# First weight chunk and x in smaller pieces on two DMA queues, with products on zeros during the loads

## Chip, cores and metric

The kernel runs on one core of a Trainium2 chip. The metric is the device time of one execution in microseconds (us).

## What is computed

One step of a two-layer decoder trunk for a prompt of 256 tokens and 8 sample tokens, 264 columns together, with 1024 features. Layer 0 mixes tokens by retention, layer 1 by a gated linear recurrence; each layer then has cross attention over a memory and a convolutional feed-forward block. All is float32. Only the beginning matters here:

```python
def trunk(x, offset, ret_s, ...):
    for i in range(DEPTH):
        hn = rmsnorm(x, p['norm_mix'][i])
        if i % N_MIXERS == 0:
            y, s = retention_mixer(hn, ret_s[j], offset, p['ret_w_in'][j], p['ret_w_out'][j])
        ...
        x = x + y
        x = x + cross_attn(rmsnorm(x, p['norm_xa'][i]), mem_k[i], mem_v[i], ...)
        y, fb = conv_ffn(rmsnorm(x, p['norm_ffn'][i]), ...)
        x = x + y

def retention_mixer(h, s0, offset, w_in, w_out):
    q, k, v, g = jnp.split(h @ w_in, [nqk, 2 * nqk, 2 * nqk + nv], axis=-1)
    ...
```

## The kernel before

Features lie on the 128 partitions, tokens along the columns. An output tile of a projection is 128 features by 264 tokens, and its sum runs over eight row tiles of 128 input features. To keep float32 precision every operand is split into two parts of fewer bits: a weight chunk `wraw` (128 x 1024 values, one output tile with its eight row tiles) is copied by ScalarE into the rounded part `wh` (`cp`, L333) and VectorE subtracts to get the rest, `wl` (`tt`, L293). The input of a projection is split in the same way: `gain` scales one row tile of x by the norm's gains on ScalarE into `A[0]` (L329) and VectorE makes the rest, `A[1]` (L299). One row tile then is three products (`mm3`): wh with the first part of A, wh with the second, wl with the first. A chunk is 24 products.

The weights form one stream of chunks, loaded through SyncE's DMA queue into six slots (`fetch`, `load` L350) and split into four slots of wh and wl (`split_next`). A load into a slot waits until the chunk in it has been split.

The order of nearly all instructions is chosen when the kernel is built: class `Clock` keeps a rough time for each engine, and a greedy planner (`one`, `process`, `until`) places background work (splits, norms, attention, stores) between the products of the main stream by these times. The main stream's order is fixed by the list `items`.

The beginning is written out by hand. `start` issues the loads and the first splits and scalings, and adds the first norm's work `g` as a background task. The first unit after it is `K.pair(*qkv[0][:2], 4)`: two output tiles, here called a (chunk 0) and b (chunk 1), in the order rows 0 to 3 of a, rows 0 to 3 of b, rows 4 to 7 of a, rows 4 to 7 of b, 48 products. Ahead of `start`, VectorE fills and copies a zeroed piece of the buffer `kvt`. The norm's factor is not needed for these products; it is multiplied in later.

Of the kernel before, what the change touches and what calls it, by code (L numbers as in the profile page):

```python
# [10 lines left out]
F32 = mybir.dt.float32  # L11
# [8 lines left out]
P = 128  # L20
D = 1024
T = 256
# [12 lines left out]

# [1 line left out]
_PRM = {}  # L37
# [17 lines left out]

# [1 line left out]
C_ID, C_ONE, C_COS, C_SIN, C_MASK = 0, P, 2 * P, 2 * P + NT, 2 * P + 3 * NT  # L57
# [113 lines left out]
class Clock:  # L171
    """A rough model of the engines' queues, by which the order of the instructions is chosen."""

# [78 lines left out]
class Kern:  # L252
# [9 lines left out]

# [1 line left out]
    @staticmethod  # L264
# [11 lines left out]
    def mm_col(self, out, lhsT, rhs, j, start, stop):  # L276
        """A product with 32 stationary columns, in column tile j of the array; four of them run side by side."""
        self.c.op("pe", 24.0 if j else max(214.0, 4 * self._n(rhs) / 2.4 + 3.0), [out], [lhsT, rhs], start)
        self.nc.tensor.matmul(out, lhsT, rhs, start=start, stop=stop, tile_position=(0, LO * j))  # L279
# [59 lines left out]
    def gain(self, m, x, g):  # L339
        """Rows x of feature tile m times its gains, split into self.A; the second half of the work returned."""  # L340
        self.act(self.A[0][:, m, :], x, AF.Identity, scale=g)
        return lambda: self.stt(self.A[1][:, m, :], x, g, self.A[0][:, m, :].bitcast(F32), MUL, SUB)
# [14 lines left out]

# [1 line left out]
    def get(self, n):  # L359
# [55 lines left out]
    def rebank(self, n):  # L415
        """From now on n banks for the main stream, the others for the background."""
        self.mgoal = n
        while self.mtot < n and self.aux:
            self.mtot += 1
            self.main.append(self.aux.popleft())  # L420
        while self.mtot > n and self.main:
            self.mtot -= 1
            self.aux.append(self.main.popleft())

# [1 line left out]
    def set_stream(self, units):  # L426
# [14 lines left out]
    def split_at(self):  # L441
        """When the next chunk of the stream can be split, as far as that is known."""
        while self.nsplit < self.nload and self.chunks[self.nsplit].raw:
            self.nsplit += 1
        if self.nsplit == self.nload or not self.hfree:
            return None
        t = max(self.chunks[self.nsplit].at, self.c.used(self.wh[:, self.hfree[0], :]))
        return max(t, self.calm(self.nsplit))

    def calm(self, n):  # L450
        """When chunk n of the stream, which is not the next to be used, may get in the way of other work."""
        d = n - self.cur
        if d < 2:
            return 0.0
        w = self.patience[min(d - 2, 1)]
        return max(self.c.t["dve"], self.c.t["act"]) - w
# [23 lines left out]
    def need(self, c):  # L480
        """Chunk c is the next of the stream to be used."""
        self.cur += 1
        self.fetch_all()
        self.until(lambda: c.rslot is not None)
        if not c.raw:
            while c.hslot is None:
                self.until(lambda: self.split_at() is not None or c.hslot is not None)
                if c.hslot is None:
                    self.split_next()
            if c.low:  # L490
                self.resume(c.low, self.now)
# [28 lines left out]

# [1 line left out]
    def add(self, gen, prio=1, at=None):  # L522
# [121 lines left out]

# [1 line left out]
    def proj(self, src, src_rhs, evac, n=NT, parts=False, tag=None):  # L646
        """The chunks in src hold the rows of one 128-feature tile, in order; with parts a unit each."""
        st = {}
# [30 lines left out]
    def pair(a, b, cut=6):  # L679
        """Two projections of one chunk each, with the last rows of the contraction of both at the end."""  # L680
        first = []
# [21 lines left out]

# [1 line left out]
    def newton(self, a, y, n, root=False):  # L705
        """y = a ** -0.5: a first guess from the exponent bits, or the root from a table, then Newton steps."""
        t = self.get(n)
# [13 lines left out]
    def rsqrt_mean(self, sq, n, cnt, wide=False, tok=None, root=False):  # L721
        """[128, n] copies of (column sums of sq / cnt + EPS) ** -0.5; a generator that returns them."""
        b = yield from self.wbank()
# [41 lines left out]
    def norm_later(self, wide=False):  # L765
        """The factors of the norm over what self.sq holds, as self.r, a few steps on."""
        gen = self.gen
# [15 lines left out]

# [1 line left out]
    def mem_units(self, l):  # L785
# [95 lines left out]

# [1 line left out]
    def retention(self):  # L883
# [237 lines left out]
    def ret_update(self, heads):  # L1121
        """New retention states of the samples: gamma * state + k v^T."""
        order = [(h, s) for h in heads for s in range(S)]
# [77 lines left out]

# [1 line left out]
    def residual(self, gain, scale=False):  # L1203
        """What becomes of the sums of output tile m: they are added to x."""
        self.gen += 1
# [48 lines left out]
    def blocks(self, plan, rows, evac):  # L1254
        """A unit for each (chunk, tiles, k): the chunk holds rows k, ... of the contraction for some output tiles."""
        bank, units, seen = {}, [], {}
# [22 lines left out]

# [1 line left out]
    def xattn(self, l):  # L1281
# [34 lines left out]
    def parts(self, src, dims):  # L1316
        """A copy of src in two parts of fewer bits that add up to it."""
        n = self._n(src)
# [73 lines left out]
    def bcast(self, src, n0):  # L1392
        """Two rows of src, n0 and n0 + 1, on all partitions of a bank."""
        b = yield from self.wbank()
# [11 lines left out]
    def samples(self, b, w, kind, l, h):  # L1406
        """Rows 32 (s % 4) + s of bank b: column s of w[:, :, s, :] times block s of the cache, over both halves."""
        ps = self.ps[:, b, :256]
# [15 lines left out]
    def gather(self, b, rows):  # L1424
        """Column s of half t of bank b: row 32 (s % 4) + s of columns 128 t to 128 t + 127 of rows."""
        for t in range(2):
# [68 lines left out]

# [1 line left out]
    def ffn(self, l):  # L1497
# [62 lines left out]

# [1 line left out]
    def lru_prep(self):  # L1562
        # 8 log_sigmoid(lam) = 8 (min(lam, 0) - log1p(exp(-|lam|))), log1p(z) = 2 artanh(z / (2 + z))
        lam = self.par[:, _PRM["lru_lambda"]:_PRM["lru_lambda"] + KD]
# [21 lines left out]
    def lru(self):  # L1586
# [3 lines left out]
        def half(name, m, n=4):  # L1590
            """Feature tile m of a buffer that is kept for half of the tiles."""
            k = (name, m // 4)
# [152 lines left out]

# How eager each part of the program is, in us: patience (2), slack of the task kinds 1 to 3, tilt, ahead.
POLICY = (
# [6 lines left out]
def tile_hybrid_step(ctx: ExitStack, tc: tile.TileContext, ins, outs):  # L1754
# [88 lines left out]
    def start():  # L1843
        K.fetch()
        nc.scalar.dma_start(out=K.par[:, :NG], in_=ins["par"][:, :NG])
        K.load(K.x[:, :4, :], ins["x"][:, :4, :])
        K.fetch()
        K.load(K.x[:, 4:, :], ins["x"][:, 4:, :])
        K.fetch()
        K.load(K.cst[:, :C_MASK], ins["cst"][:, :C_MASK])  # L1850

        def split():
            c = K.chunks[K.nsplit]
            K.split_next()
            K.resume(c.low, K.now)
        split()
        K.load(K.cst[:, C_MASK:], ins["cst"][:, C_MASK:])
        K.load(K.par[:, NG:], ins["par"][:, NG:])
        for m in range(KD):
            K.gain(m, K.x[:, m, :], K.prm("norm_mix", m))()  # L1860
            K.ready.add(("A", 0, m))
            if m == 3:
                split()
        split()

# [35 lines left out]
    def staged(units, n):  # L1901
        """The last part of each of the first n tiles comes after the other parts of all of them."""
        out = [u for us in units[:n] for u in us[:-1]] + [us[-1] for us in units[:n]]
        return out + [u for us in units[n:] for u in us]
# [9 lines left out]
    def out(w, plan, rows, gain):  # L1914
        """plan: what to wait for, or chunks of w."""
        ev = K.blocks([c for st in plan if isinstance(st, list) for c in st], rows, K.residual(gain))
# [131 lines left out]
```

## Time and profile before

| | us |
|---|---|
| median of 3 runs | 1046.58 |
| lowest and highest run | 1046.05 to 1047.74 |
| span of the profiled execution (first to last instruction) | 1044.7 |
| own time of the profiled execution | not listed apart from the three runs |
| TensorE busy | 1023.0 |
| VectorE busy | 807.4 |
| ScalarE busy | 589.4 |

The profiled execution is one run of the program recorded by the hardware profiler. Its span leaves out what lies before the first and after the last instruction; the median is 1.9 us above it. PE is TensorE's matmul, PEld its weight load, DVE is VectorE, ACT ScalarE, SP SyncE; L274 is line 274 of the kernel. The ends of matmuls are modelled, so the distance between the starts of two rows tells their pace better than their durations do.

### The profile page before, as it was taken

How to read it: one execution, taken by the hardware profiler on the slowest of the kernel's cores; microseconds unless marked ns; L12 is line 12 of the kernel's file. 1: busy time of each engine (PE TensorE's matmuls, PEld its weight loads, DVE VectorE, ACT ScalarE, POOL GpSimd, SP SyncE). 2: the span in 40 equal slices, each digit the busy share in tenths (PEclk: the TensorE clock that was granted, in tenths of full speed). 3: DMA queues.
4: the chain of work that ended last, by engine and by line, in shares of the span. 5: the costliest groups of instructions: out<-in, count | busy, mean ns of one | idle time of the engine just before them, and what ended most of it. 6: DMA issues, size and time to landing. Idle time of an engine off the chain costs nothing.

```text
span 1044.7 us, 20974 instructions
## 1 busy us (share of the span) xinstructions
PE 1023.0 (98%) x8158; PEld 966.4 (93%) x8158; DVE 807.4 (77%) x1685; ACT 589.4 (56%) x979; POOL 84.4 (8%) x190
## 2 busy tenths in 40 slices
PE   7999999999999999999999999999999999999996
PEld 7988999889998868999999999999878999999996
DVE  7968788777677644898988776989755898898773
ACT  6554555455545434575676554697444666766552
POOL 0000000000000000023221000400000222121000
PEclk9999999999999999999999999999999999999998
DMA  9667766774766897567888977546886668777851
GB/s 371 207 216 248 272 224 232 263 262 164 271 218 235 297 315 256 191 212 259 266 297 291 301 235 233 172 164 233 311 286 223 209 203 290 272 256 272 299 192 62
DMA packets 70916, 255.45 MB, mean 245 GB/s; under 512 B 8096, under 2 KB 8736, under 8 KB 70304
## 3 DMA queue, kind: packets, MB, share of 16 engines
q1 hardware_dynamic: 70384, 253.53, 70.4%
q8 instruction: 64, 1.05, 0.4%
q10 hardware_dynamic: 432, 0.58, 0.2%
q14 instruction: 36, 0.29, 0.1%
HBM read 229.34 MB, written 24.74 MB: 243 GB/s over the span
## 4 chain that ended last, share of the span: by engine, by line
PE 87%; DVE 6%; DMA 3%; ACT 3%; issue 1%; SPq 0%; DVEq 0%; ACTq 0%
PE ps L274 83%; PE ps L279 3%; DVE wl L293 2%; DVE x L299 2%; DVE x L293 1%; DMA kvt<-in_cache_v 1%; DMA x<-in_cache_k 1%; ACT x L329 1%; PE ps L289 1%; ACT L329 1%; ACT wh L333 1%; DMA kvt<-in_cache_k 1%; DVE x L318 0%; DMA wraw<-in_ret_w_in 0%; DVE B L293 0%
## 5 line engine op out<-in xcount | busy, mean ns | idle before, releaser
L274 PE MATMUL ps<-A,wh 128*128 128x264 f32 x2816 | 525.1, 287 | 7.1 <-ACT A L329 6.3
L333 ACT CAST wh<-wraw 128x1024 fp32r<-128x1024 f32 x284 | 297.2, 1049 | 281.3 <-PE ps L274 237.2
L274 PEld LDWEIGHTS ps<-A,wh 128*128 128x128 f32 x2816 | 437.2, 189 | 16.0 <-ACT A L329 6.3
L293 DVE TENSOR_TENSOR wl<-wraw,wh 128x1024 fp32r<-128x1024 f32 x296 | 359.2, 1220 | 93.4 <-ACT wh L333 85.6
L274 PE MATMUL ps<-A,wl 128*128 128x264 f32 x1408 | 400.1, 284 | 0.1
L274 PE MATMUL ps<-B,wh 128*128 128x264 f32 (+1 forms) x1664 | 311.8, 288 | 2.2 <-DVE B L293 2.2
L274 PEld LDWEIGHTS ps<-B,wh 128*128 128x128 f32 x1664 | 257.3, 188 | 12.7 <-issue 8.6
L274 PEld LDWEIGHTS ps<-A,wl 128*128 128x128 f32 x1408 | 265.1, 188 | 0.4 <-DVE wl L293 0.3
L274 PE MATMUL ps<-B,wl 128*128 128x264 f32 (+1 forms) x832 | 235.5, 283 | 0.0
L274 PEld LDWEIGHTS ps<-B,wl 128*128 128x128 f32 x832 | 156.2, 188 | 0.0
L293 DVE TENSOR_TENSOR x<-ps,x 128x264 f32<-128x264 f32 (+2 forms) x248 | 83.9, 364 | 33.1 <-PE ps L274 21.2
L337 POOL COPY x<-x 128x16 f32<-128x16 f32 (+2 forms) x162 | 78.3, 518 | 268.1 <-DVE x L293 217.2
L329 ACT ACTIVATE x<-x 128x264 f32<-128x264 f32 (+4 forms) x166 | 59.7, 389 | 20.2 <-DVE x L293 8.7
L299 DVE SCALAR_TENSOR_TENSOR x<-x,par 128x280 f32<-128x280 f32 (+3 forms) x128 | 61.5, 488 | 2.3
L333 ACT COPY x<-ps 128x512 f32<-128x512 f32 (+3 forms) x85 | 39.2, 475 | 42.0 <-PE ps L274 31.2
L299 DVE SCALAR_TENSOR_TENSOR kvt<-x,vst,kvt 128x256 f32<-128x256 f32 x128 | 53.3, 477 | 1.3 <-ACT kvt L329 1.3
L299 DVE SCALAR_TENSOR_TENSOR junkt<-kvt,x 128x256 bf16<-128x256 f32 x128 | 46.4, 420 | 9.1 <-DMA kvt<-in_state_ret 6.4
L293 DVE TENSOR_TENSOR x<-x 128x264 f32<-128x264 f32 (+6 forms) x106 | 44.8, 435 | 7.7 <-ACT x L329 5.8
L333 ACT CAST B<-x 128x264 fp32r<-128x264 f32 (+2 forms) x84 | 34.7, 417 | 24.5 <-DVE x L293 17.4
L329 ACT ACTIVATE x<-x,par 128x280 f32<-128x280 f32 (+2 forms) x64 | 38.6, 605 | 8.9 <-DVE x L293 5.9
L293 DVE TENSOR_TENSOR B<-x,B 128x264 fp32r<-128x264 f32 (+2 forms) x84 | 36.7, 438 | 8.4 <-ACT B L333 8.2
L274 PE MATMUL ps<-wh,B 128*128 128x512 f32 x128 | 42.5, 400 | 0.0
(100 smaller groups left out, 703.6 us busy)
## 6 DMA issues: line engine op xcount, KB each, us to landing
wraw<-in_ffn_w_up SPq DMA_DIRECT2D x96, 512.0 KB, 4.4
kvt<-in_state_ret SPq DMA_DIRECT2D x64, 512.0 KB, 6.0
wraw<-in_ret_w_in SPq DMA_DIRECT2D x48, 512.0 KB, 4.4
wraw<-in_ffn_w_down SPq DMA_DIRECT2D x48, 512.0 KB, 4.7
out_ret_s<-kvt SPq DMA_DIRECT2D x32, 512.0 KB, 5.1
x<-in_cache_v SPq DMA_DIRECT2D x18, 512.0 KB, 6.7
wraw<-in_xa_w_k SPq DMA_DIRECT2D x16, 512.0 KB, 4.4
wraw<-in_xa_w_v SPq DMA_DIRECT2D x16, 512.0 KB, 4.1
```

Of the source, the lines that this page charges most:

```text
L274: self.last = self.nc.tensor.matmul(out, lhsT, rhs, start=start, stop=stop)
L279: self.nc.tensor.matmul(out, lhsT, rhs, start=start, stop=stop, tile_position=(0, LO * j))
L289: self.nc.tensor.transpose(out, in_, self.ident[:n, :n])
L293: self.nc.vector.tensor_tensor(out=out, in0=a, in1=b, op=op)
L299: self.nc.vector.scalar_tensor_tensor(out, a, s, b, op0, op1, **kw)
L329: self.nc.scalar.activation(out, in_, func, **kw)
L333: self.nc.scalar.copy(out, in_)
L337: self.nc.gpsimd.tensor_copy(out, in_)
```

## The change

In `start`, five float32 products of 128 x 128 with 128 x 256 on a zeroed part of `kvt` are put ahead of everything, into a PSUM bank that nothing uses then. Chunk 0 is loaded in three pieces (row tiles 0 and 1, 2 and 3, 4 to 7), x in three (row tiles 0 and 1 through ScalarE's queue; 2 and 3, then 4 to 7 through SyncE's). The pieces of chunk 0 are split one by one, each followed by the scalings of its row tiles of x. Chunks 1 and 2 are split after that. Chunk 1 is now issued behind all of x, and the constants go ahead of chunk 2. The pair's order is the same. The rest of the diff removes comments.

```diff
     def start():
-        K.fetch()
+
+        zero = kvt[:, 0, :512]
+        nc.vector.memset(zero, 0.0)
+        for _ in range(5):
+            K.mm(K.ps[:, 7, :256], zero[:, :P], zero[:, P:P + 256], True, True, False)
+        c = K.chunks[0]
+        c.rslot, c.hslot = K.rfree.popleft(), K.hfree.popleft()
+        K.nload = K.nsplit = 1
+        cuts = (0, 256, 512, 1024)
+        parts = [slice(a, b) for a, b in zip(cuts, cuts[1:])]
+        raw, wh, wl = (t[:, n, :] for t, n in ((K.wraw, c.rslot), (K.wh, c.hslot), (K.wl, c.hslot)))
         nc.scalar.dma_start(out=K.par[:, :NG], in_=ins["par"][:, :NG])
-        K.load(K.x[:, :4, :], ins["x"][:, :4, :])
-        K.fetch()
+        K.load(raw[:, parts[0]], c.src[:, parts[0]])
+        nc.scalar.dma_start(out=K.x[:, :2, :], in_=ins["x"][:, :2, :])
+        K.load(raw[:, parts[1]], c.src[:, parts[1]])
+        K.load(K.x[:, 2:4, :], ins["x"][:, 2:4, :])
+        c.at = K.load(raw[:, parts[2]], c.src[:, parts[2]])
         K.load(K.x[:, 4:, :], ins["x"][:, 4:, :])
         K.fetch()
         K.load(K.cst[:, :C_MASK], ins["cst"][:, :C_MASK])
-
-        def split():
+        K.fetch()
+        m = 0
+        for n, p in enumerate(parts):
+            K.cp(wh[:, p], raw[:, p])
+            K.tt(wl[:, p], raw[:, p], wh[:, p].bitcast(F32), SUB)
+            for m in range(cuts[n] // P, cuts[n + 1] // P):
+                K.gain(m, K.x[:, m, :], K.prm("norm_mix", m))()
+                K.ready.add(("A", 0, m))
+        K.rfree.append(c.rslot)
+        K.fetch()
+        K.load(K.cst[:, C_MASK:], ins["cst"][:, C_MASK:])
+        K.load(K.par[:, NG:], ins["par"][:, NG:])
+        for _ in range(2):
             c = K.chunks[K.nsplit]
             K.split_next()
             K.resume(c.low, K.now)
-        split()
-        K.load(K.cst[:, C_MASK:], ins["cst"][:, C_MASK:])
-        K.load(K.par[:, NG:], ins["par"][:, NG:])
-        for m in range(KD):
-            K.gain(m, K.x[:, m, :], K.prm("norm_mix", m))()
-            K.ready.add(("A", 0, m))
-            if m == 3:
-                split()
-        split()
```

## Rows read from the trace of the kernel before

**Rows 1.** The page, busy us of each engine, share of the span, instructions.

```profile
PE 1023.0 (98%) x8158; PEld 966.4 (93%) x8158; DVE 807.4 (77%) x1685; ACT 589.4 (56%) x979; POOL 84.4 (8%) x190
```

**Rows 2.** The chain that ended last: start us, us, what.

```profile
7.05 27.24 PE ps L274 x206
```

**Rows 3.** TensorE's waits: us in total, times, longest us.

```profile
PE ps L274 <- ACT A L329: 6.3, 1, 6.3
PE ps L274 <- DVE B L293: 2.2, 2, 1.7
PE ps L274 <- DVE sq L293: 1.9, 1, 1.9
PE ps L279 <- DMA x<-in_cache_k: 1.7, 2, 1.4
PE ps L274 <- DVE x L299: 1.3, 1, 1.3
```

**Rows 4.** Windows: length, busy us by engine, granted clock, DMA share, GB/s.

```profile
0.00:5.00 5.00, 0.00 (x0) 0.00 (x0) 1.94 (x3) 2.00 (x2) 0.20 (x4) 1.00 0.62 222
5.00:10.00 5.00, 3.54 (x14) 3.24 (x15) 4.15 (x7) 4.20 (x9) 0.00 (x0) 1.00 1.01 394
...
12.00:300.00 288.00, 288.00 (x2145) 270.20 (x2143) 224.05 (x583) 148.89 (x236) 3.01 (x5) 1.00 0.71 249
```

**Rows 5.** Timeline of TensorE: start us, us, instruction, [idle before it <- releaser].

```profile
6.30 0.59 PE L274 MATMUL ps<-A,wh 128*128 128x264 f32 x1 [6.30 <-ACT A L329]
7.05 0.59 PE L274 MATMUL ps<-A,wh 128*128 128x264 f32 x1 [0.16 <-DVE A L299]
...
11.02 0.64 PE L274 MATMUL ps<-A,wh 128*128 128x264 f32 x2
11.46 0.35 PE L274 MATMUL ps<-A,wl 128*128 128x264 f32 x1
...
12.00 0.41 PE L274 MATMUL ps<-A,wh 128*128 128x264 f32 x2
...
14.93 0.41 PE L274 MATMUL ps<-A,wh 128*128 128x264 f32 x2
```

**Rows 6.** Timeline of ScalarE.

```profile
4.28 1.04 ACT L333 CAST wh<-wraw 128x1024 fp32r<-128x1024 f32 x1 [1.83 <-DMA wraw<-in_ret_w_in]
5.73 1.73 ACT L329 ACTIVATE A<-x,par 128x264 fp32r<-128x264 f32 x4 [0.40 <-DMA x<-in_x]
7.62 1.05 ACT L333 CAST wh<-wraw 128x1024 fp32r<-128x1024 f32 x1 [0.15 <-DMA wraw<-in_ret_w_in]
8.91 1.74 ACT L329 ACTIVATE A<-x,par 128x264 fp32r<-128x264 f32 x4 [0.24 <-DMA x<-in_x]
```

**Rows 7.** Timeline of VectorE.

```profile
1.02 0.91 DVE L1790 MEMSET kvt<- 128x1024 f32 x1 [1.02 <-PEq L2026]
...
2.57 0.42 DVE L1812 CAST f<-kvt 128x512 fp32r<-128x512 f32 x1
...
8.70 1.22 DVE L293 TENSOR_TENSOR wl<-wraw,wh 128x1024 fp32r<-128x1024 f32 x1 [0.49 <-ACT wh L333]
...
11.61 1.23 DVE L293 TENSOR_TENSOR wl<-wraw,wh 128x1024 fp32r<-128x1024 f32 x1
```

**Rows 8.** Timeline of TensorE, products of plain float32 operands.

```profile
79.10 1.88 PE L274 MATMUL ps<-x 128*128 128x512 f32 x4
```

**Rows 9.** Windows over the closing norm, columns as in rows 4.

```profile
1034.00:1036.00 2.00, 0.83 (x6) 0.74 (x6) 0.77 (x4) 0.57 (x2) 0.00 (x0) 0.89 0.00 0
1036.00:1038.00 2.00, 1.45 (x6) 1.35 (x6) 0.33 (x3) 0.06 (x1) 0.00 (x0) 0.50 0.00 0
```

**Rows 10.** Timeline of TensorE around a wait for a load.

```profile
372.84 1.06 PE L279 MATMUL ps<-x 128*32 128x256 f32 x12 [1.38 <-DMA x<-in_cache_k]
...
374.17 0.28 PE L274 MATMUL ps<-B,wl 128*128 128x256 f32 x1
374.28 0.28 PE L274 MATMUL ps<-f 128*128 128x256 f32 x1
```

## The prediction

> **What bounds the kernel now.** I read the page's busy shares first, then the chain that ended last, then TensorE's waits, and then each engine's timeline over the first 16 us. TensorE is busy for 98% of the span [rows 1]. The chain is one unbroken TensorE piece from 7.05 to 34.29 us [rows 2], so an early start or a late one goes into the end one for one as long as nothing later takes it up. TensorE's waits are 6.3 us before its first product, and then 7.1 us in its four next groups [rows 3]. Of these the 1.9 and 1.3 us stand in the closing norm (its sq product and the one after it); the other 3.9 us lie after 300 us, since from 12 to 300 us it is never idle [rows 4].
>
> The front has two parts that could give time back. TensorE begins at 6.30 us, and until 11.46 us it runs at half speed: from 11.02 to 11.46 us two products take 0.44 us, 0.22 each, while from 12.00 to 14.93 us 24 products take 2.93 us, 0.122 each [rows 5]. The granted clock reads 1.00 there all the same [rows 4], so in this stretch the spacing tells the level (1.2 GHz, then 2.4) and the record doesn't. Counting the rows from 6.30 us, 24 products are through at 12.00 us and all 48 of the first pair at 14.93 us. That second moment is my yardstick: the next tile starts there, and its chunk was split long before.
>
> Who sets those moments? ScalarE waits for the first chunk until 4.28 us and for x until 5.73; it starts chunk 1 at 7.62 and the second half of x at 8.91, each after a short wait for the DMA [rows 6]. VectorE follows at once: the chunk 1 difference starts at 8.70 and ends at 9.92 [rows 7].
>
> **The change, part by part.**
>
> *Bytes.* A chunk is 128 x 1024 x 4 bytes, 512 KB; half of x is 528 KB. Before, the order is chunk 0, x first half, chunk 1, x second half. Chunk 1 was thus complete after 1552 KB, at 7.6 us, and the second half of x after 2080 KB, at 8.9 us [rows 6]. After the change all of chunk 0 and all of x go ahead of chunk 1: the second half of x is complete after 1568 KB, chunk 1 after 2080 KB. The two change places: x at 7.6 us, chunk 1 at 8.9 us. The stream moves 394 GB/s with the DMA engines fully busy [rows 4], so more pieces cannot pull both ahead.
>
> The first half of x now goes partly through ScalarE's queue, and the trace has no two large streams side by side. The Trainium skill, DMA: Bandwidth & Descriptors, section Issuing engines are not separate DMA queues, says that both queues run on the same 16 engines and that a second one saves only issue time; that speaks against a gain, and by it the sum stays as below. If the 264 KB came free of the other stream instead, everything behind would land 0.69 us sooner, and the lower bound below would hold.
>
> *First products.* Tile a's first four rows need only the first two pieces and x's first half, so their products can start earlier than 6.30 us, by the bytes at some 5 us. They don't, because of the zeros.
>
> *Zeros.* VectorE's last fill work ends at 2.99 us; the new memset has half the columns of the first (0.91 us) [rows 7], so it takes 0.45 to 0.91 us and the five products start at 3.5 to 3.9 us. Their operands are plain float32, which shows as two rows a product; four rows of 512 columns took 1.88 us at full speed [rows 8], so 0.235 a row of 256, 2.35 us for the ten rows, and 4.7 at half speed. They end between 5.8 and 8.6 us; I take 8.2. Twelve products of tile a follow, 0.122 to 0.22 each, and are through at 9.7 to 10.8 us.
>
> *Chunk 1 behind the scalings.* This is the term that decides. The pair still runs four rows of tile a and then four of tile b, and tile b is chunk 1. But ScalarE now has all pieces of chunk 0 and all eight scalings ahead of chunk 1's copy. The last four scalings start when x is there, 7.6 us, and take 1.74; the copy of chunk 1 takes 1.05 more, to 10.4; VectorE's difference 1.22, to 11.65 [rows 6, 7]. Of tile b's first three products the first two need the copy, the third the difference: it starts at 11.7 us. From there 34 products are left (48 - 12 - 2), all their other inputs ready: 34 x 0.122 = 4.15 us at full speed. The pair ends at 11.7 + 4.15 = 15.85 us against 14.93: **0.9 us later**. What the zeros gain, 24 products at half speed no longer there, is spent waiting for chunk 1.
>
> *Bounds.* Below: ScalarE must do four scalings (0.43 each) and two pieces (some 0.8) after the first quarter of x, which is 520 KB down the stream, so about the 4.28 us of chunk 0: it is free at 6.8 us at the soonest. If x is there by then, everything is 0.8 us sooner, and the pair ends at 15.05, 0.1 us later. Above: the small pieces have rows of 1 and 2 KB where the trace has 4 KB. If they moved at the 222 GB/s of the first 5 us [rows 4], the 1040 KB before the last half of x would take 4.8 us instead of 2.7, 2.1 us later: 3.0 us in all. I take 0.9, since the 394 GB/s row is the nearer; in the 222 the DMA engines are busy for only 0.62 of the time.
>
> *The rest.* Three copies and three differences for one of each, another memset, one more ScalarE issue of some 0.4 us: all on engines that wait at that point, so nothing. If that cover were gone, they are some 0.6 us. Behind the chunk 1 copy on ScalarE stand the chunk 2 split and the squares of the first norm. Chunk 2 now has 524 KB of constants ahead of it: 1036 KB behind chunk 1, 2.7 us at 394 GB/s, it is there at 11.6 us, its copy done at 12.65 and its difference at 13.9, for a use that is now at 15.85. Before, the difference ended at 12.84 for a use at 14.93 [rows 5, 7]: the same 2 us in hand. The other constants now pass SyncE's queue ahead of chunk 4; that chunk is used two tiles after chunk 2, at 21.8 us, and those 780 KB are 2.0 us of the stream. The total of bytes is the same.
>
> *The planner.* All else is placed at build time by the kernel's clock model. Its times move with the new front, and later background work may take other places. Between 12 and 300 us TensorE has no wait to win back; after that it has the 3.9 us [rows 3, 4]. I take zero for this and keep plus or minus 1 us for the forecast's own range.
>
> **Sum.** The profiled execution spans 1044.7 us; its own time is not listed, and the median of the runs, 1046.58, lies 1.9 us above. 1044.7 + 0.9 + 1.9 = 1047.5 us. About 0.2%, 2.1 us, is what a measurement of this kernel can tell from no change.
>
> **Rivals.**
> 1. *Clock falls back.* TensorE idles at 9.7 to 10.4 and again until 11.7 us. In the closing norm, with 0.83 us of products in 1034 to 1036 us, the granted clock went from 0.89 there to 0.50 [rows 9]. Against it: a 1.4 us wait at 371 us left products at the full rate, 0.11 us from one start to the next [rows 10], and here more products stand ahead of the gaps. The Trainium skill, TensorE: Matmul & The Clock Gate, section What's actually happening, has the throttled state as the default that activity releases; the closing rows agree. Price: before, half speed lasted from 7.05 to 11.46 us; 4.4 x (1 - 0.122/0.22) = 2.0 us. Sum +2.9: 1049.5. Chance 0.15.
> 2. *New waits after 300 us.* The planner's other order adds a wait like the largest group it has, 2.2 us: 0.9 + 2.2 = +3.1, 1049.7. For: VectorE is close behind TensorE for long. Against: 288 us without a wait show slack [rows 4]. Chance 0.15.
> 3. *Other side: the new order takes waits away.* Place: the 3.9 us after 300 us, waits for cache loads and for the B split [rows 3]. From 3.0 us taken away it decides (0.9 - 3.0 = -2.1); with all gone it gives 0.9 - 3.9 = -3.0, 1043.6. Chance 0.14. The front alone cannot do it by these rows: even at its lower bound it is 0.1 us later.
> 4. *No effect:* the lower bound holds and the order stays, 1046.7. Chance 0.11.
>
> **Numbers.** Forecast 0.45: 1047.5, own range 1046.1 to 1048.6. Slower by over 0.2% hold rivals 1 and 2, 0.30; faster rival 3 and a little, 0.15; the rest, 0.55, is within 0.2%. The range for 8 in 10 runs from 1044.9 (half of the other side's case left out) to 1050.2 (the upper front bound of 3.0 us with some reordering).
>
> **What would show it.** In the changed profile: zeros from 3.5 us; tile a's products at full spacing from about 8 us; TensorE waiting for chunk 1's wh and then wl, the third product of tile b at 11.7 us; the pair's end at 15.85; spacing 0.122 after the gap. If tile b starts by 9.5 us, my byte order is wrong; if the spacing after the gap is 0.22, rival 1 holds; if the pair ends as forecast but the total differs by more than 2 us, the planner did it, and the waits after 300 us must say where.

## The result and the profile after

The changed kernel takes 1055.45 us (median of six runs, 1050.15 to 1057.49) against 1047.16 for the kernel before in the same session: 1.0063 times, 95% interval 1.0046 to 1.0079. A later session with twelve runs of it gave 1052.42 us against 1047.74, 1.0036 (1.0022 to 1.0050). It is slower in both, by 6.6 and 3.8 us by these ratios (8.3 and 4.7 by the medians), and both medians lie above the range that was forecast.

The first six runs go with the granted clock that each lists as its mean: 1050.15 us at 0.997, 1050.89 at 0.996, then 1054.81 to 1057.49 at 0.993 to 0.991. The twelve later ones lie between 1050.70 and 1054.53 at 0.997 to 0.993. So two profiles of the same kernel are read here: the first, 1056.96 us with a span of 1055.2 at 0.992, and the repeat, 1052.5 us with a span of 1050.7 at 0.996. The span before was 1044.7, at 0.996 too.

TensorE's waits in the first profile (us in total, times, longest). Those for wl, 2.3 us in one piece, and for wh weren't there before [rows 3]; those for the caches have grown. The line for in_cache_v stands below for the kernel before too, and then the two for the repeat:

```profile
PE ps L274 <- DVE kvt L1846: 3.7, 1, 3.7
PE ps L279 <- DMA x<-in_cache_k: 3.1, 2, 1.8
PE ps L274 <- DVE wl L293: 3.1, 2, 2.3
...
PE ps L279 <- DMA kvt<-in_cache_v: 1.0, 3, 0.4
PE ps L274 <- ACT wh L333: 0.8, 1, 0.8
```

```profile
PE ps L279 <- DMA kvt<-in_cache_v: 0.4, 1, 0.4
```

```profile
PE ps L279 <- DMA x<-in_cache_k: 2.2, 2, 1.5
...
PE ps L279 <- DMA kvt<-in_cache_v: 1.5, 3, 0.8
```

The front on TensorE, first profile (start, us, instruction, idle before it and its releaser):

```profile
3.71 4.63 PE L274 MATMUL ps<-kvt 128*128 128x256 f32 x10 [3.71 <-DVE kvt L1846]
...
9.88 0.28 PE L274 MATMUL ps<-A,wl 128*128 128x264 f32 x1
...
11.33 0.51 PE L274 MATMUL ps<-A,wh 128*128 128x264 f32 x2 [0.81 <-ACT wh L333]
12.59 0.39 PE L274 MATMUL ps<-A,wl 128*128 128x264 f32 x1 [0.75 <-DVE wl L293]
...
13.78 0.64 PE L274 MATMUL ps<-A,wh 128*128 128x264 f32 x2
14.22 0.42 PE L274 MATMUL ps<-A,wl 128*128 128x264 f32 x1
...
18.38 0.41 PE L274 MATMUL ps<-A,wh 128*128 128x264 f32 x2
```

The pair ends at 18.38 us; before it was 14.93 [rows 5]. The two waits for chunk 1 come in the forecast order, wh and then wl, and end 0.9 us later than forecast (12.59 instead of 11.7). From 13.78 to 14.22 us two products take 0.44, 0.22 each: half speed again, after it had been full. ScalarE shows who was late:

```profile
5.10 0.92 ACT L329 ACTIVATE A<-x,par 128x264 fp32r<-128x264 f32 x2 [0.76 <-DMA x<-in_x]
...
8.61 1.74 ACT L329 ACTIVATE A<-x,par 128x264 fp32r<-128x264 f32 x4 [0.69 <-DMA x<-in_x]
10.25 1.03 ACT L333 CAST wh<-wraw 128x1024 fp32r<-128x1024 f32 x1
```

The last four scalings wait for x until 8.61 us (forecast 7.6). Chunk 1's copy follows them without a wait for its load. Windows of the same profile, columns as in [rows 4], give the stream's rate and the granted clock at three places where it fell:

```profile
0.00:5.00 5.00, 1.29 (x3) 1.12 (x4) 2.85 (x5) 1.69 (x2) 0.21 (x4) 1.00 0.55 172
5.00:10.00 5.00, 5.00 (x17) 4.28 (x17) 3.57 (x9) 4.04 (x10) 0.00 (x0) 1.00 0.97 369
...
14.00:16.00 2.00, 2.00 (x11) 2.00 (x11) 1.27 (x2) 2.00 (x3) 0.00 (x0) 0.50 1.03 401
...
34.00:36.00 2.00, 1.87 (x8) 1.88 (x9) 2.00 (x5) 0.80 (x1) 0.00 (x0) 0.50 0.99 272
36.00:38.00 2.00, 2.00 (x14) 2.00 (x13) 2.00 (x4) 0.00 (x0) 0.00 (x0) 0.71 0.81 264
725.00:730.00 5.00, 4.60 (x25) 4.61 (x26) 4.85 (x7) 2.54 (x4) 0.81 (x1) 0.66 0.43 136
```

The 2.3 us wait comes at 32 us, in the stretch that had none [rows 4]. TensorE and then VectorE, first profile:

```profile
31.36 0.46 PE L274 MATMUL ps<-A,wh 128*128 128x264 f32 x2
34.13 0.59 PE L274 MATMUL ps<-A,wl 128*128 128x264 f32 x1 [2.31 <-DVE wl L293]
```

```profile
26.11 0.69 DVE L465 CAST wh<-wraw 128x1024 fp32r<-128x1024 f32 x1
28.24 0.98 DVE L293 TENSOR_TENSOR cst<-cst,x 128x792 f32<-128x792 f32 x1 [1.43 <-ACT x L333]
29.26 2.55 DVE L293 TENSOR_TENSOR x<-ps,cst 128x528 f32<-128x528 f32 x4
31.73 3.48 DVE L293 TENSOR_TENSOR wl<-wraw,wh 128x1024 fp32r<-128x1024 f32 x3
```

The same stretch of VectorE in the kernel before:

```profile
22.66 1.22 DVE L293 TENSOR_TENSOR wl<-wraw,wh 128x1024 fp32r<-128x1024 f32 x1
24.78 0.98 DVE L293 TENSOR_TENSOR cst<-cst,x 128x792 f32<-128x792 f32 x1 [0.90 <-ACT x L333]
25.80 2.55 DVE L293 TENSOR_TENSOR x<-ps,cst 128x528 f32<-128x528 f32 x4
28.26 2.35 DVE L293 TENSOR_TENSOR wl<-wraw,wh 128x1024 fp32r<-128x1024 f32 x2
```

Before, chunk 6's difference runs at 22.66 us, ahead of the scaling of the constants (cst) and four evacuations. After, the planner has put VectorE's copy of chunk 7 there (26.11), and the difference of chunk 6 is the second of the three at 31.73, behind chunk 7's: it ends at 34.07, when TensorE goes on (34.13). Each of these steps is as long as before; their order is new. ScalarE's copy of chunk 6 has moved too, from 3.0 us behind the pair's end to 7.9, behind a copy (rtok) that waits for VectorE. Before, then after:

```profile
17.91 1.05 ACT L333 CAST wh<-wraw 128x1024 fp32r<-128x1024 f32 x1 [1.16 <-PE ps L274]
```

```profile
26.23 0.19 ACT L333 COPY rtok<-x 128x2 f32<-128x2 f32 x1 [6.71 <-DVE x L299]
26.32 1.04 ACT L333 CAST wh<-wraw 128x1024 fp32r<-128x1024 f32 x1
```

In the repeat, TensorE has the same waits and the clock stays up. Its rows, and its windows below:

```profile
8.39 0.28 PE L274 MATMUL ps<-A,wl 128*128 128x264 f32 x1
8.51 0.41 PE L274 MATMUL ps<-A,wh 128*128 128x264 f32 x2
...
12.69 0.39 PE L274 MATMUL ps<-A,wl 128*128 128x264 f32 x1 [0.75 <-DVE wl L293]
...
16.92 0.41 PE L274 MATMUL ps<-A,wh 128*128 128x264 f32 x2
...
32.66 0.39 PE L274 MATMUL ps<-A,wl 128*128 128x264 f32 x1 [2.31 <-DVE wl L293]
```

```profile
14.00:16.00 2.00, 2.00 (x19) 2.00 (x18) 1.26 (x2) 2.00 (x3) 0.00 (x0) 1.00 1.04 405
...
34.00:36.00 2.00, 2.00 (x19) 1.93 (x18) 2.00 (x5) 0.46 (x1) 0.00 (x0) 1.00 0.80 244
```

So the two spans can be added up against 1044.7. Repeat: pair's end 16.92 - 14.93 = 2.0; the wait 2.3; the waits for the cache loads 3.7 instead of 2.1, so 1.6. That is 5.9 of 6.0. First profile: pair's end 3.45 (of it 34 products in 5.79 us instead of 4.15: 1.64 at half speed); the wait 2.3; half speed behind it 1.87 x 0.50 + 2.00 x 0.29 = 1.5; half speed at 725 us 4.60 x 0.34 = 1.6; cache loads 2.0. That is 10.9 of 10.5. The two profiles differ by 4.5 us, nearly all of it clock (1.64 + 1.5 + 1.6 = 4.7).

### The profile page after: what moved, and what is told of

Same layout as the page of the kernel before. It is cut to its first block, busy times and chain, and to the rows that moved or that the text cites. A ratio compares the mean times of both kernels' runs of the same rounds, so it can differ in the third digit from the quotient of the medians.

```text
span 1055.2 us, 20997 instructions
## 1 busy us (share of the span) xinstructions
PE 1030.5 (98%) x8168; PEld 972.2 (92%) x8168; DVE 809.0 (77%) x1688; ACT 589.0 (56%) x981; POOL 85.4 (8%) x190
## 4 chain that ended last, share of the span: by engine, by line
PE 86%; DVE 6%; DMA 4%; ACT 3%; issue 1%; SPq 0%; DVEq 0%; ACTq 0%
PE ps L274 82%; PE ps L279 3%; DVE wl L293 2%; DVE x L293 2%; DVE x L299 1%; DMA kvt<-in_cache_v 1%; DMA x<-in_cache_k 1%; ACT x L329 1%; PE ps L289 1%; ACT L329 1%; ACT wh L333 1%; DMA x<-in_x 1%; DMA kvt<-in_cache_k 1%; DVE x L318 0%; SPq L350 0%
## 5 line engine op out<-in xcount | busy, mean ns | idle before, releaser
L333 ACT CAST wh<-wraw 128x1024 fp32r<-128x1024 f32 (+1 forms) x286 | 297.8, 1043 | 284.1 <-PE ps L274 225.7
L293 DVE TENSOR_TENSOR wl<-wraw,wh 128x1024 fp32r<-128x1024 f32 (+1 forms) x298 | 359.4, 1213 | 91.2 <-ACT wh L333 85.7
L329 ACT ACTIVATE x<-x 128x264 f32<-128x264 f32 (+3 forms) x162 | 58.2, 388 | 20.3 <-DVE x L293 8.9
```

Of the source, the lines that this page charges most:

```text
L293: self.nc.vector.tensor_tensor(out=out, in0=a, in1=b, op=op)
L329: self.nc.scalar.activation(out, in_, func, **kw)
L333: self.nc.scalar.copy(out, in_)
```

## The experiments

Theory O: the larger part is the planner's new order behind the front, with the wait near 32 us at its core. Its rivals put the loss into the front (theory F: late chunk 1, the zeros, the second queue) or into the clock behind the front's gaps.

**Front and order apart.** `unseen` issues a front without moving the planner's clock; `planned` moves the clock and issues nothing (`front_a` is the changed `start`, `front_b` the old one). The first run has the new front and the old order behind it, the second the old front and the new order.

```diff
+    def start():
+        unseen(front_a)    # e1; e2: unseen(front_b)
+        planned(front_b)   # e1; e2: planned(front_a)
```

> The changed front runs, but the planner is given the times of the old front, so all that follows the first pair has the order of the kernel before. Theory F (the front itself: chunk 1 behind the scalings, the clock falling in the gap, and TensorE then late against an order made for an earlier one): the pair ends at 16.5 to 18.4 us, 1.5 to 3.5 us late, and the wait at some 32 us comes too, since the norm's product is late on TensorE: 1052 to 1056 us. Theory O (the planner's new order makes the wait at 32 us): that wait is gone and only the lateness of the front stays: 1048.5 to 1051 us.

> The old front runs, but the planner is given the times of the changed front, so all that follows the first pair has the order of the changed kernel. Theory F: no wait of over 0.5 us at 32 us, and 1046 to 1048 us, as before. Theory O: TensorE waits some 2 us near 30 us although the pair ends at 14.9, with a clock fall behind it in some runs: 1049 to 1052 us.

The front alone: 1050.76 us against 1047.61, 1.0030 (1.0014 to 1.0046). The order alone: 1049.68, 1.0017 (1.0002 to 1.0032). One window of the first and one of the second:

```profile
32.00:34.00 2.00, 2.00 (x19) 2.00 (x18) 2.00 (x6) 2.00 (x3) 0.00 (x0) 1.00 0.82 260
```

```profile
28.00:30.00 2.00, 0.11 (x1) 0.00 (x0) 2.00 (x3) 2.00 (x4) 0.00 (x0) 1.00 0.02 4
```

With the old order TensorE is busy through 32 to 34 us, though the front is late (its pair ends at 16.79 us). With the new order and the old front the pair ends at 14.67 us, and still TensorE stands still for 2.3 us from 28.1. The DMA engines stand still with it: SyncE's queue waits 9.8 us for a chunk's difference, by which a slot comes free, and issues its next load at 29.25. The order makes that wait, not the front. That the order is the larger part of the time, as theory O has it, isn't shown: the two factors multiply to 1.0047, between the two sessions of the whole change, and the front's is the bigger of the two, with intervals that overlap.

**Without the zeros, and with tile a run whole first.**

```diff
-        K.mm(K.ps[:, 7, :256], zero[:, :P], zero[:, P:P + 256], True, True, False)  # e3, x5
-    K.pair(*qkv[0][:2], 4)
+    K.pair(*qkv[0][:2], 8)                                                      # e4
```

> The changed kernel without its five products on zeros (which nothing uses), all other instructions in the same order. Theory F with the zeros of no use: tile a starts at 5.7 us at half speed, tile b still waits for chunk 1 to 12.6 us, and half speed lasts beyond it: the pair ends at 17 to 19 us, and the time is that of the changed kernel, 1053 to 1057 us. Rival: the zeros keep the clock up in part of the runs, then without them every run is like the slow ones, 1055 to 1058. Second rival: the zeros themselves hold TensorE up, then it is faster than the changed kernel by 2 us or more, below 1053.

> One number: the first pair does all eight rows of tile a before tile b, so TensorE has work while chunk 1 is split. If chunk 1 behind the scalings is the cause of the gap and of the clock fall: tile a runs to some 11 us, the third product of tile b still starts at 12.6, the clock holds, and the pair ends at 15.3 us, some 3 us sooner than in the changed kernel. The wait at 32 us then shrinks or goes (theory F, 1047 to 1050 us) or stays at 2 us (theory O, 1050 to 1053 us).

Without the five products (all else in the changed order): 1053.19 us, 1.0050 (1.0032 to 1.0069). With all of tile a ahead of tile b: 1052.30, 1.0041 (1.0025 to 1.0057). By these times neither can be told from the change itself. Tile b's third product and the pair's end in the first, and the third product in the second:

```profile
12.21 0.58 PE L274 MATMUL ps<-A,wl 128*128 128x264 f32 x1 [0.76 <-DVE wl L293]
...
17.98 0.41 PE L274 MATMUL ps<-A,wh 128*128 128x264 f32 x2
```

```profile
12.41 0.39 PE L274 MATMUL ps<-A,wl 128*128 128x264 f32 x1 [0.35 <-DVE wl L293]
```

Without zeros tile a starts at 5.50 us, and tile b waits for chunk 1 all the same, until 12.21. The 34 products from there take 5.77 us instead of 4.15, a part of them at half speed, and the pair ends at 17.98; with the zeros it ended at 16.92 in the repeat and at 18.38 in the first profile. So the zeros don't shorten the wait, and whether they bring anything for the clock behind it, one profile doesn't show. With tile a whole, 22 products instead of 34 are left at 12.41 us, the pair ends at 15.17, 0.2 behind the kernel before, and the total is still 2.6 to 6.0 us above it. The 2.3 us wait is in both profiles. That speaks for the order.

**Gap filled.** The run with the front alone, and four more products on zeros between tile a's and tile b's first rows.

```diff
+    for _ in range(4):
+        nc.tensor.matmul(K.ps[:, 7, :256], zero[:, :P], zero[:, P:P + 256], start=True, stop=True)
```

> The changed front with the old order behind it (as in the run of the front alone), and four more products on zeros, used by nothing, between tile a's and tile b's first rows. Theory clock: they keep the clock up across the gap, so every run has full spacing after 12.6 us and the pair ends at 16.7 us in all of them: 1048.5 to 1050, at least 1 us under the front alone. Theory chunk 1 (its place in the queues is the whole cost, the clock little): within 0.7 us of the front alone, 1050 to 1051.5.

1048.79 us against 1047.73, 1.0020 (1.0007 to 1.0032). The time is the one that theory clock expected, some 1 us under the front alone, but the intervals overlap, and the two runs stand in different sessions. The profiles don't show the clock as its cause: the pair ends at 16.56, 0.2 sooner than with the front alone (16.79), but chunk 1's difference was 0.25 sooner too (third product of tile b at 12.32 instead of 12.57), and the 34 products from there take 4.2 us, full speed, in both. The mean granted clock of the runs is 0.9955 instead of 0.9948.

**Chunk 1 first, zeros first.** All three keep the old order. Run e6 loads and splits chunk 1 ahead of chunk 0's last piece and x's second half. e7 is the kernel before with the five products on the zeros that were there already, without a memset of their own. e8 is both.

```diff
+    K.fetch()                                                          # e6, e8: chunk 1
     K.load(raw[:, parts[2]], c.src[:, parts[2]])
...
+    if n == 2:
+        K.split(K.wh[:, 1, :], K.wl[:, 1, :], K.wraw[:, d.rslot, :])   # e6, e8
-    nc.vector.memset(zero, 0.0)                                        # e8; e7 has none
```

> The changed front with one thing undone: chunk 1 is loaded ahead of chunk 0's last piece and of x's second half and split ahead of their work, as the first pair uses it. Old order behind it. If chunk 1's place is the term: no gap, the zeros end at 8.3 us and set the start, the pair ends at 14.2 us (0.7 us before the old front), 1046 to 1047.5 us. If the pieces themselves are slow, tile b or tile a's second half still waits over 1 us and it is 1049 or more.

> The kernel before, with the five products on zeros alone, on the zeros that the first fill writes, no second fill, same order. If they bring what they are for: zeros from 2 to 6.3 us, full spacing from the first products on, tile b held by chunk 1's difference at 9.95 us, pair ends at 14.1 us, 0.8 us sooner: 1046 to 1047. If the wait for chunk 1 swallows all: 14.9 us and the time of before, 1047 to 1048.

> Chunk 1 early, and the zeros without their second fill, so that they start at 2 us: both repairs. Zeros end at 6.3 us, tile a's first rows are through by 8 us, tile b's third product starts at some 9.4, the pair ends at 13.0 to 13.5 us: 1.5 to 2 us under the kernel before, 1045 to 1046.5. Rival: chunk 2's difference, needed at 13 us, comes at 13.5 to 14 and takes 0.5 to 1 us back: 1046 to 1047.

The pair ends at 14.30, 13.97 and 13.66 us, 0.6 to 1.3 sooner than before. The row at that point, in this order:

```profile
14.30 0.41 PE L274 MATMUL ps<-A,wh 128*128 128x264 f32 x2
```

```profile
13.97 0.41 PE L274 MATMUL ps<-A,wh 128*128 128x264 f32 x2
```

```profile
13.66 0.40 PE L274 MATMUL ps<-A,wh 128*128 128x264 f32 x2
```

The times are 1048.18 (1.0011, 1.0002 to 1.0020), 1047.11 (1.0001, 0.9987 to 1.0014) and 1047.55 (1.0001, 0.9990 to 1.0013), against 1047.73. So the front's deciding term is confirmed: with chunk 1 ahead, the pair comes 2.5 us sooner than with the front alone (14.30 for 16.79), and the time goes from 1.0030 to 1.0011, with intervals that just overlap. But no gain in the front was seen in the total: e6 and e8 miss the times expected of them (1046 to 1047.5 and 1045 to 1046.5), and e6 is slower than the kernel before although its pair ends sooner. In the last two profiles the waits for cache loads are larger than before (4.7 and 4.4 us together, 2.1 before); one profile each does not show that this is where the microsecond went.

**One queue.** The changed kernel, with x's first quarter on SyncE's queue.

```diff
-    nc.scalar.dma_start(out=K.x[:, :2, :], in_=ins["x"][:, :2, :])
+    K.load(K.x[:, :2, :], ins["x"][:, :2, :])
```

> The changed kernel with x's first quarter on SyncE's queue too, all other instructions in the same order. If the second queue moves nothing ahead: x's first quarter, chunk 1 and the gap stand within 0.3 us of the changed kernel's places and the time is the changed kernel's, 1052 to 1056. If the second queue carries the quarter beside the stream, then without it tile a's scalings start later than 5.1 us by 0.3 or more; if it delays the weight pieces, chunk 1 comes sooner without it and the gap shrinks by 0.3 us or more.

1053.90 us against 1047.58, 1.0057 (1.0038 to 1.0075): by the time no different. But the places moved by more than 0.3 us, and not in the way of any of the cases above. ScalarE's first scalings, and those of x's last half:

```profile
4.26 0.92 ACT L329 ACTIVATE A<-x,par 128x264 fp32r<-128x264 f32 x2 [0.39 <-DMA x<-in_x]
...
9.55 1.73 ACT L329 ACTIVATE A<-x,par 128x264 fp32r<-128x264 f32 x4 [0.96 <-DMA x<-in_x]
```

Through the second queue the first piece came for 5.10 us, and the last half for 8.61; in the eight profiles with these loads on two queues the last half came for 8.20 to 8.71. So with one queue the first quarter is sooner, and the last half 0.8 us or more later: tile b's third product starts at 13.53 instead of 12.59. In the first two windows of 5 us the stream moves 150 and 328 GB/s instead of 172 and 369. The second queue does not explain the late stream; in this one profile the stream is later still without it.

**The planner's step.** Run e10 is the changed kernel with chunk 6's difference issued as soon as its copy is. e11 holds only chunk 7's copy on ScalarE. e12 is the changed kernel itself.

```diff
         self.tasks.append(c.low)
+        if c is self.chunks[6]:                                            # e10
+            self.resume(c.low, self.now)
...
-        if self.c.t["act"] > self.c.t["dve"] + self.tilt:
+        if c is not self.chunks[7] and self.c.t["act"] > self.c.t["dve"] + self.tilt:  # e11
```

> The changed kernel with one step of the planner overruled: chunk 6's difference on VectorE is put right behind its copy, ahead of the scaled constants and the four evacuations, as in the order of the kernel before; 183 of 4834 TensorE entries of the order differ by it. If that one step makes the wait at 32 us: no wait of over 0.5 us there, no clock fall behind it, and 2 to 4 us less than the changed kernel: 1049.5 to 1052. If the wait only moves (to the next chunk, or to the banks that the evacuations free), 1052.5 to 1056.

> The changed kernel, with chunk 7's copy held on ScalarE. In the changed kernel's program that copy is on VectorE, and chunk 7's difference stands ahead of chunk 6's there. Theory O has two parts, and this run tells them apart. If the copy's place alone makes the wait, chunk 6's difference comes back ahead of the constants' scaling and the wait near 32 us is gone: some 1050 us. If the decisive part is that the planner puts both differences behind the constants' scaling and the four evacuations, only chunk 7's difference (1.2 us) leaves the queue ahead of chunk 6's, the second copy on ScalarE (1.05 us) delays the scaling by some 0.6, and TensorE still waits 1.7 us instead of 2.3: some 0.6 us less than the changed kernel, not to be told from it. I expect the second.

> The changed kernel unaltered, in the session of the run above, to have its spread: theory O expects the 2.3 us wait near 32 us in its profile again, and a time 5 to 8 us above the kernel before. If its granted clock stays up at 13 us in this profile, the pair ends near 16.8 us instead of 18.38.

With chunk 6's difference first: 1050.32 us against 1047.58, 1.0025 (1.0012 to 1.0038). With chunk 7's copy on ScalarE: 1051.84 against 1047.74, 1.0028 (1.0015 to 1.0042). The changed kernel beside it: 1052.42, 1.0036. VectorE in e10, then TensorE in e11:

```profile
25.43 1.23 DVE L293 TENSOR_TENSOR wl<-wraw,wh 128x1024 fp32r<-128x1024 f32 x1 [1.21 <-ACT wh L333]
26.66 0.98 DVE L293 TENSOR_TENSOR cst<-cst,x 128x792 f32<-128x792 f32 x1
```

```profile
31.50 0.39 PE L274 MATMUL ps<-A,wl 128*128 128x264 f32 x1 [1.17 <-DVE wl L293]
```

In e10 the wait is gone, and its span (1047.2) is 3.5 us below the repeat's: 0.5 from the front, 2.3 from the wait and 1.3 from cache loads are 4.1, so 0.6 is lost elsewhere. ScalarE's copy of chunk 6 is as late in e10 as in the changed kernel (7.9 us behind the pair's end), so that copy alone doesn't make the wait. In e11 half of it goes (1.17 left; I had expected 1.7): chunk 7's difference no longer stands ahead of chunk 6's, and both still stand behind the constants and the evacuations. So the wait is made of two steps of VectorE's order, some 1.2 us each. By the times alone the three can't be told apart.

## Why the prediction was wrong

By the two runs that part them, the front cost 3.1 us of time (1.0030) where the forecast had 0.9, and the order 1.8 (1.0017) where it had nothing. The first is a term of the sum that was too small, the second a term that was put at nothing.

**Byte order, and chunk 1 as the deciding term: right.** TensorE waits for wh and then for wl of chunk 1, at 11.33 and 12.59 us, and moving chunk 1 ahead brings the pair 2.5 us forward.

**The time of x: mis-sized.** The copies, scalings and differences took what was forecast. But x's last half was taken for complete at 7.6 us and came at 8.6 to 8.7 in these two profiles (8.20 to 8.71 in eight), so the third product was at 12.59 and 12.69 instead of 11.7. The windows show the stream behind: 172 GB/s in the first 5 us against 222 is 250 KB less, and 369 against 394 up to 8.6 us another 90 KB; 340 KB are 0.9 us at 394 GB/s. I had kept this for the upper bound and taken zero. In the repeat the pair ends at 16.92, 2.0 late instead of 0.9. That the small pieces make the stream slower is the explanation left, since the second queue doesn't; it is argued and not shown, as pieces of another size weren't tried.

**"Between 12 and 300 us TensorE has no wait to win back" and "288 us without a wait show slack": the step that failed.** From no wait I read slack. The busy row tells nothing of it. Chunk 6's tile starts 13.0 us behind the pair's end (31.36 behind 18.38). In the kernel before that is 27.91 us, and its third product, 0.3 later, needs the difference, which ended at 23.88: 4.3 us in hand.

```profile
28.20 0.28 PE L274 MATMUL ps<-A,wl 128*128 128x264 f32 x1
```

In the new order the difference ends 15.7 us behind the pair's end (34.07 behind 18.38) instead of 8.95. That is 6.7 us later and 2.4 too late, the 2.3 us that stand in every profile with the unaltered new order, with the old front too. Rival 2 had a new wait of just this size, but looked for it after 300 us and got 0.15. Which estimate in the planner's clock tipped the order of chunk 6 wasn't traced; that of chunk 7's copy is worth half of it.

**Clock.** Full spacing was forecast from about 8 us: it came at 8.39 in the repeat and at 9.88 in the first profile. Rival 1's fall behind the gap came in the first profile, at the predicted half speed and for 1.64 us (forecast 2.0), and again behind the wait at 32 us and at 725 us; in the repeat at none of these places. The Trainium skill, TensorE: Matmul & The Clock Gate, section What's actually happening, has half speed as the default that activity releases; the rows after each of the three idle pieces agree, and the repeat shows that such a piece doesn't always bring it. By the listed clocks (span times one minus the clock) the first six runs lost 6.7 us on the mean, the twelve of the repeat's session 5.0, the kernel before 4.8. So the clock is some 1.7 of the 3.0 us between the two medians, and hardly a part (0.2) of the repeat's 4.7 us.

**The second queue.** The sum gave it no gain; a gain was priced at 0.69 us and left to the lower bound. By the time the run with one queue was no slower, but in its profile x's last half came 0.9 us later, which is nearer to the gain. The Trainium skill, DMA: Bandwidth & Descriptors, section Issuing engines are not separate DMA queues, has all issuers share the same 16 engines, with only the time of issuing saved by a second one. That profile doesn't bear this out: the load of x's last half is issued 0.48 us later in it (3.06 instead of 2.58 us) and lands 0.9 later, and the DMA engines are as busy (shares of 0.53 and 1.00 in the first two windows, 0.55 and 0.97 with two queues) at a lower rate. It is one profile; why the rate was lower stays open.

**What stays open:** where the waits for cache loads come from (2.1 us before, 3.7 and 4.1 with the change, 1.0 in e11), where the front's time beyond the pair's lateness goes (3.1 us against 1.9 in its profile), and why the clock falls in one execution and not in another with the same gaps.

## What to carry to other kernels

When an order is planned from modelled times, an edit at the start changes it far behind; the forecast then has to read, for each step that feeds the busy engine, how long before its use it ends, since a span without waits doesn't tell that. Separate the two with a run that issues one front and plans by the other: here it split a change of some 5 us into a late front and a reordered queue. And work ahead of a wait doesn't shorten the wait if that is for a load that the same edit has moved back.

## What the hardware showed unexpectedly

The recorded clock reads 1.00 in the first 10 us of both profiles, while products run at 0.22 us, half speed, until 8.4 or 9.9 us; later falls are recorded as 0.50. Behind a wait of 1.69 us for the B split, which ended at 725.40 us, the clock was 0.66 over 5 us in the first profile. In the kernel before the same wait, as long, ended at 716.39 us, and the clock stayed at 1.00 in the window behind it:

```profile
716.00:721.00 5.00, 4.61 (x37) 4.61 (x38) 4.93 (x7) 3.43 (x5) 0.81 (x1) 1.00 0.41 134
```

In the repeat it ended at 721.82 us after 1.68, and the 5 us behind it read 1.00.

A piece of x of 264 KB issued on a second queue came 0.8 us later than through the queue that already carried the chunks (5.10 and 4.26 us), and the pieces behind it came sooner (x's last half for 8.61 and 9.55 us), in one profile with one queue.
